# A hybrid decoder layer on one core: the weight ring's pool, the dt chain, the sparse rows and the ada sums change places

## The chip, the cores and the metric

The kernel runs on one core of a Trainium2 chip. The metric is device time in microseconds, from the start to the end of one execution; the number given for a kernel is the median of several runs. A core has five engines with a queue of instructions each, which run in order: PE (TensorE, matrix multiplication into PSUM), DVE (VectorE), ACT (ScalarE), POOL (GpSimd) and SP (SyncE, which here only issues transfers). An engine that reaches an instruction whose input is not there waits, and all behind it in its queue waits too. PEld is TensorE's weight load.

## The reference

One layer over 512 tokens of width 2048, in float32:

```
mod = silu(c) @ W_ada + b_ada            # six vectors of 2048: sh1, sc1, g1, sh2, sc2, g2
h = rmsnorm(x) * (1 + sc1) + sh1
c_q, c_kv, k_rope, z, xBC, dt_raw = split(h @ W_in)
attn = rmsnorm(MLA attention over c_q, c_kv, k_rope)      # 8 heads, causal
dt = softplus(dt_raw + dt_bias); cs = cumsum(-exp(a_log) * dt) inside chunks of 128
ssm = grouped rmsnorm(SSD over xBC, dt, gated with z)      # 16 heads, 4 chunks
x = x + g1 * (concat(attn, ssm) @ W_out)
h2 = rmsnorm(x) * (1 + sc2) + sh2
# PEER: 8 heads, each with two sets of 128 sub-keys
q = h2 @ W_query; top 16 of 128 in each half; top 16 of the 256 sums -> 16 of 16384 experts
x = x + g2 * sum over the chosen experts of gate * gelu(u_e . h2) * v_e
```

## The kernel before

Activations lie with features on the 128 partitions and the 512 tokens along the row. A float32 product is made of three matmuls: each factor is split into a rounded high part and a low rest (`mm`, lines 134 to 137). Weights come through a ring: `wload` (139 to 149) takes a raw buffer, loads it on SP's queue, makes the high part on ACT (147) and the low part with `sub_lo` on POOL or DVE (130, 148). `big` (151) calls it for eight rows of tiles at a time. The ring's pool is replaceable (`wpool`): "wp" with 4 raw and 2 + 2 part buffers of 4 KB up to line 766, "we" with 5 raw and 3 + 3 after it.

The stages, in the order of the program text: the first norm and the six latent tiles of w_in (274 to 316), rotary tables and latents (319 to 368), the late tiles of w_in (374 to 394), the projections of the first four heads (729), three weaves of attention, SSD, first half of w_out and the rest (731 to 735), the second half of w_out (739 to 748), the second norm (753 to 766), product-key selection (814 to 847), the spread of gates into a dense table (943 to 944), early expert rows (945), sparse rows (947 to 955), and the main loop over 128 groups of experts (1029 to 1059).

A framework orders each engine's queue: it takes the program text's order as priority and fills an engine with the first instruction that its timing model takes to be ready. So an instruction may run long before or after its place in the text. `tc.issue_after(ins)` puts what follows behind a given instruction of the same engine; `pace` holds the last matmul, the last DVE step and so on for that.

Pools are stacks on two sides of the on-chip memory. A pool that is opened after another was closed takes over its addresses, and a tile there waits for the old tiles that it overlaps (`reuse_waits="tile"`). At line 766 the left side is closed down to the constants; on it had stood, in this order, the ring "wp" (32 KB a partition), the small tiles of "ep" (9 KB), 28 pages of "pb" (2 KB each, among them the 16 tiles x1), and "tpp" with the norm's tiles h2t and h2k.

The ada stream. `ada_stream` (232 to 271) is a generator that computes 16 pieces of the vector `mod` on DVE: eight loads of 512 KB each per piece into two buffers (240, on SP), a multiplication with accumulation per half load (263, 265), and at step 3 of the next piece the sum over partitions, which is four transposes on PE (`colsum`, 172, tile adat), a reduction (174) and `ada_done`. Each step is pulled by `next(later)` after a piece of other work.

The dt chain (563 to 597) turns the dt columns of w_in into dt, adt, and by two small matmuls csp (588) and csl (592) into cumulative sums; SSD needs its results.

Selection (780 to 847): per query half a w_q tile, an evacuation qt (831), four score matmuls scp (834), five DVE searches per 128 tokens (839 to 843); per head a second round over the 256 sums, `cand` (786 to 795), and one-hot sums (809 to 812). The copies of h2 for the main loop into h2hi and h2lo are lines 844 and 845.

The spread (909 to 939): for groups of 32 tokens, one-hot tiles oi and oj on DVE, POOL and ACT, matmuls gps (930), copies gt on ACT (933) and writes of gd to memory from ACT's queue (937). The first 160 tokens (NS) are not computed densely; their rows of h2, written to memory as h2b in the norm (761), come back transposed as h2t and h2x (947 to 955): five loads on ACT's queue (950), 32 transposes h2p (954), eight copies (955). The main loop reads gd back as gc on SP (1035), between the loads of expert weights; x1s, loaded at 770, is the residual to which it adds from line 1057 on.

## Time and profile before

| | |
|---|---|
| time, median of 3 runs | 3273.81 us (3272.5 to 3276.46) |
| the profiled execution | 3275.95 us, its span 3274.2 us |
| busy share of the span | PE 93%, PEld 86%, DVE 78%, ACT 36%, POOL 30% |
| from about 1391 us to the end | the main loop, PE without a pause |

The profile is of one execution. A timeline row has start and duration in us, engine, line, operation, output and inputs, shapes and count; in square brackets the idle time of the engine ahead of it and what ended that. SPq and ACTq are transfers issued from the queues of SP and ACT. A table by stretches gives the busy time of every engine in each stretch, the granted clock of TensorE (1.00 is 2.4 GHz, 0.50 is 1.2 GHz) and the share and rate of the transfer engines. A row of the waits says which engine and line waited for which, the sum in us, how often, and the longest.

### The profile page before, as it was taken

The numbers are of one execution on the slowest core, as the hardware profiler recorded it, in microseconds if no ns is written. First come the engines' busy times: TensorE is split into PE (matmuls) and PEld (weight loads), VectorE is DVE, ScalarE is ACT, GpSimd is POOL, SyncE is SP. The second block draws the span as 40 slices with busy tenths as digits, with TensorE's granted clock in tenths as the row PEclk, the third lists the DMA queues.
The fourth block names the chain that finished last, engine by engine and source line by source line (L and its number), as shares of the span: only waits on it lengthen the run. The fifth ranks groups of instructions, "written<-read, shape, count | busy, mean of one in ns | idle before, by whom it ended". The sixth has DMA issues, their size and how long they took to land.

```text
span 3274.2 us, 46175 instructions
## 1 busy us (share of the span) xinstructions
PE 3058.9 (93%) x17753; PEld 2804.6 (86%) x17753; DVE 2539.3 (78%) x3844; ACT 1172.0 (36%) x1796; POOL 994.9 (30%) x701
## 2 busy tenths in 40 slices
PE   5998988889949989799999999999999999999999
PEld 2476766567837789799999999999999999999999
DVE  3257677787749999678888888888888888888885
ACT  2242235642242248633333333333333333333332
POOL 1143335544435665422222222222221121211210
PEclk8999999999969999899999999999999999999999
DMA  8636753438642236879998998998998998998994
GB/s 317 244 98 218 238 193 105 127 106 303 205 134 83 89 109 182 228 278 374 340 340 319 351 339 321 346 345 321 346 340 329 341 339 330 339 342 331 338 332 130
DMA packets 286844, 858.78 MB, mean 262 GB/s; under 512 B 35872, under 2 KB 96416, under 8 KB 245664
## 3 DMA queue, kind: packets, MB, share of 16 engines
q1 hardware_dynamic: 169024, 480.13, 41.7%
q0 software_dynamic: 46080, 335.56, 27.5%
q10 hardware_dynamic: 71520, 40.15, 4.2%
q8 instruction: 139, 2.28, 0.3%
q14 instruction: 81, 0.66, 0.1%
HBM read 816.65 MB, written 39.06 MB: 261 GB/s over the span
## 4 chain that ended last, share of the span: by engine, by line
PE 58%; DVE 6%; ACT 3%; DMA 1%; issue 1%; POOL 1%; ACTq 1%; SPq 0%; DVEq 0%; POOLq 0%
PE pv L137 10%; PE pv L135 10%; PE pv L136 10%; PE up L137 9%; PE up L135 9%; PE up L136 9%; ACT gt L933 1%; PE gps L930 1%; DMA gd<-gt 1%; DVE eq L809 0%; DVE slots L812 0%; DVE topi L843 0%; DVE sc L841 0%; DVE topi L840 0%; ACT oi L922 0%
## 5 line engine op out<-in xcount | busy, mean ns | idle before, releaser
L137 PE MATMUL up<-h2hi,ul 128*128 128x352 f32 x2048 | 665.3, 325 | 0.1
L135 PE MATMUL up<-h2hi,uh 128*128 128x352 f32 x2048 | 663.5, 324 | 0.4 <-ACT uh L147 0.4
L135 PE MATMUL pv<-ah,vh 128*128 128x352 f32 x2048 | 659.6, 323 | 3.1 <-ACT ah L1040 2.1
L136 PE MATMUL up<-h2lo,uh 128*128 128x352 f32 x2048 | 662.1, 323 | 0.0
L136 PE MATMUL pv<-al,vh 128*128 128x352 f32 x2048 | 661.0, 323 | 0.0
L137 PE MATMUL pv<-ah,vl 128*128 128x352 f32 x2048 | 657.1, 323 | 1.0 <-DVE vl L130 1.0
L147 ACT ACTIVATE vh<-vr 128x1024 fp32r<-128x1024 f32 x256 | 271.8, 1062 | 624.0 <-PE pv L136 539.2
L147 ACT ACTIVATE uh<-ur 128x1024 fp32r<-128x1024 f32 x256 | 271.4, 1061 | 557.8 <-PE up L136 418.5
L130 DVE TENSOR_TENSOR vl<-vr,vh 128x1024 fp32r<-128x1024 f32 x256 | 312.8, 1223 | 187.7 <-ACT vh L147 187.5
L130 POOL TENSOR_TENSOR wl<-wr,wh 128x1024 fp32r<-128x1024 f32 (+2 forms) x134 | 293.6, 2196 | 449.6 <-ACT wh L147 354.2
L130 DVE TENSOR_TENSOR ul<-ur,uh 128x1024 fp32r<-128x1024 f32 x230 | 281.3, 1223 | 145.5 <-ACT uh L147 145.5
L137 PEld LDWEIGHTS up<-h2hi,ul 128*128 128x128 f32 x2048 | 389.5, 190 | 0.4 <-DVE ul L130 0.4
L135 PEld LDWEIGHTS pv<-ah,vh 128*128 128x128 f32 x2048 | 385.6, 188 | 3.8 <-ACT ah L1040 2.5
L135 PEld LDWEIGHTS up<-h2hi,uh 128*128 128x128 f32 x2048 | 385.7, 188 | 0.7 <-ACT uh L147 0.7
L136 PEld LDWEIGHTS up<-h2lo,uh 128*128 128x128 f32 x2048 | 386.2, 189 | 0.0
L137 PEld LDWEIGHTS pv<-ah,vl 128*128 128x128 f32 x2048 | 384.6, 188 | 1.3 <-DVE vl L130 1.3
L136 PEld LDWEIGHTS pv<-al,vh 128*128 128x128 f32 x2048 | 385.4, 188 | 0.1
L981 POOL DMA_INDIRECT g<-u_r,idx x128 | 166.7, 1302 | 574.1 <-DVE acc L999 466.0
L981 POOL DMA_INDIRECT g<-v_t,idx x128 | 147.4, 1151 | 573.2 <-DVE pre L987 550.9
L999 DVE SCALAR_TENSOR_TENSOR acc<-g,cf,acc 128x2048 f32<-128x2048 f32 x127 | 297.8, 2345 | 0.0
L987 DVE CUSTOM_DVE_ANT_0 g<-g,h2t 128x2048 f32<-128x2048 f32 x128 | 292.1, 2283 | 2.4 <-DMA g<-u_r,idx 2.4
L147 ACT ACTIVATE wh<-wr 128x1024 fp32r<-128x1024 f32 (+2 forms) x134 | 126.7, 949 | 347.4 <-PE pj L136 76.4
(443 smaller groups left out, 4985.0 us busy)
## 6 DMA issues: line engine op xcount, KB each, us to landing
ur<-u_t SPq DMA_DIRECT2D x256, 512.0 KB, 6.6
vr<-v_d SPq DMA_DIRECT2D x256, 512.0 KB, 6.1
wada<-w_ada SPq DMA_DIRECT2D x128, 512.0 KB, 4.1
wada<-w_ada SPq DMA_DIRECT2D x128, 256.0 KB, 5.3
gd<-gt ACTq DMA_DIRECT2D x22, 1024.0 KB, 8.3
gc<-gd SPq DMA_DIRECT2D x32, 704.0 KB, 8.5
wr<-w_in SPq DMA_DIRECT2D x40, 512.0 KB, 4.9
wr<-w_out SPq DMA_DIRECT2D x32, 512.0 KB, 5.7
```

What stands on the lines that cost most here:

```text
L130: return eng.tensor_tensor(lo, src, hi.bitcast(F32), ALU.subtract)
L135: nc.tensor.matmul(ps, a[0], b[0], start=start, stop=False)
L136: nc.tensor.matmul(ps, a[0], b[1], start=False, stop=False)
L137: pace[5] = nc.tensor.matmul(ps, a[1], b[0], start=False, stop=stop)
L147: nc.scalar.activation(hi[:, :n], raw[:, :n], AF.Copy)
L930: pace[2] = nc.tensor.matmul(ps[:, t * P:(t + 1) * P], oi[:, t], oj[:, t], start=True, stop=True)
L933: nc.scalar.activation(gt[:, :, t4_ * 4:t4_ * 4 + 4].rearrange("p j t -> p t j"), pv_[:, :, jh * 64:(jh + 1) * 64], AF.Copy)
L981: nc.gpsimd.indirect_dma_start(out=g, out_offset=None, in_=table, in_offset=bass.IndirectOffsetOnAxis(ap=ix[:, s - s0:s - s0 + 1], axis=0))
L987: nc.vector.tensor_tensor_reduce(g, g, rows, 1.0, 0.0, ALU.mult, ALU.add, accum_out=pre[:, s:s + 1])
L999: nc.vector.scalar_tensor_tensor(acc, g, cf[:, s:s + 1], acc, op0=ALU.mult, op1=ALU.add)
```

## The change

Five things. The new ring's pool "we" is opened ahead of "p5", and x1s is no tile of "p5" any more: it is allocated, and loaded, in the main loop's pool. The dt chain stands behind the latents, ahead of the late tiles of w_in. The sum of an ada piece is made at step 6 of the next piece, not 3. The sparse rows are read after the second of three spread tiles, with a buffer of their own (one) in place of the three of gt. And cand and qt get a second buffer.

```diff
-            if i % 8 == 3 and ended:
+            if i % 8 == 6 and ended:
                 with tc.issue_after(pace[5].ins):
                     ada_done(*ended[:2], colsum(ended[2], "ada"))
...
     cq = latent(cq, "qa", 512, "rq")
+    def stile(name):
+        return ep.tile([P, NT, 16], F32, name=name)
+    dt, ax, ay, az, adt = stile("dt"), stile("ax"), stile("ay"), stile("az"), stile("adt")
...
+    nc.scalar.activation(sdec, sdec, AF.Exp)
...
-    (the same lines, from def stile to sdec, ahead of ys, rS)
...
     left.close()
+    wpool.update(pool=ctx.enter_context(pool("we")), raw=5, parts=3)
     p5 = ctx.enter_context(pool("p5"))
-    wpool.update(pool=ctx.enter_context(pool("we")), raw=5, parts=3)
-    x1 = p5.tile([P, KD, TD], F32, name="x1s")
-    nc.scalar.dma_start(x1, x1d[:, :, NS:].rearrange("k p t -> p k t"))
     h2 = [p5.tile([P, KD, TD], F32R, name=n) for n in ("h2hi", "h2lo")]
...
-        cand = lp.tile([P, NT, 16, 16], F32, tag="cand", name="cand", bufs=1)
+        cand = lp.tile([P, NT, 16, 16], F32, tag="cand", name="cand")
...
-        qt = lp.tile([P, T], F32, tag="qt", name="qt", bufs=1)
+        qt = lp.tile([P, T], F32, tag="qt", name="qt")
...
+    def sparse_rows():
+        for dst, t0, n in ((h2t, 0, P), (h2x, P, XT)):
+            h0 = rp.tile([P, KD, P], F32, name="h2f", bufs=1)
+            for q in range(P // n):
+                nc.scalar.dma_start(h0[:, :, q * n:(q + 1) * n], h2b[:, :, t0:t0 + n].rearrange("k p t -> p k t"))
+            for q in range(4):
+                ps = gpp.tile([P, T], F32, tag="g", name="h2p")
+                for j in range(4):
+                    nc.tensor.transpose(ps[:, j * P:(j + 1) * P], h0[:, q * 4 + j], ident)
+                nc.scalar.activation(dst[:, q * T:(q + 1) * T], ps, AF.Copy)
     for tt in (1, 2, 3):
         spread(tt, by_slot(tt))
+        if tt == 2:
+            sparse_rows()
     ges = {j: up(j) for j in range(EARLY)}
-    (the old loop over h2t and h2x, with tag="gt", bufs=3)
...
     pe_ = ctx.enter_context(pool("pe", 2))
+    x1 = pe_.tile([P, KD, TD], F32, name="x1s", bufs=1)
+    nc.scalar.dma_start(x1, x1d[:, :, NS:].rearrange("k p t -> p k t"))
```

## Rows read from the trace of the kernel before

**Rows 1.** Stretches: us; busy PE, PEld, DVE, ACT, POOL; clock, DMA, GB/s.
```profile
920.00:940.00 20.00, 0.00 (x0) 0.00 (x0) 18.34 (x26) 10.88 (x18) 9.30 (x6) 0.50 0.35 102
...
1000.00:1020.00 20.00, 20.00 (x92) 16.31 (x91) 20.00 (x84) 5.56 (x9) 14.11 (x6) 1.00 0.26 88
...
1260.00:1280.00 20.00, 19.64 (x153) 19.36 (x152) 20.00 (x60) 18.66 (x44) 13.53 (x16) 1.00 0.54 163
```

**Rows 2.** Waits of PE, whole span: sum in us, times, longest.
```profile
PE wq L135 <- ACT wh L147: 41.0, 1, 41.0
...
PE adat L172 <- DVE acc L263: 15.6, 6, 5.5
PE h2p L954 <- DMA h2f<-h2b: 15.3, 1, 15.3
PE scp L834 <- ACT qt L831: 12.3, 3, 7.9
...
PE csl L592 <- DVE cs L589: 8.8, 1, 8.8
```

**Rows 3.** Timeline of SP, ACT and PE around the first w_q tiles.
```profile
930.32 1.62 SPq L146 DMA_DIRECT2D wr<-w_q  x2
...
937.16 0.48 ACT L844 ACTIVATE h2hi<-h2h 128x352 fp32r<-128x352 f32 x1
...
949.50 1.65 ACT L147 ACTIVATE wh<-wr 128x512 fp32r<-128x512 f32 x3
...
950.17 0.79 PE L135 MATMUL wq<-h2h,wh 128*128 128x512 f32 x1 [41.03 <-ACT wh L147]
...
972.99 0.58 ACT L831 ACTIVATE qt<-wq 128x512 f32<-128x512 f32 x1
```

**Rows 4.** Timeline of DVE and POOL in the second norm.
```profile
920.33 0.42 DVE L763 CAST h2h<-h2k 128x512 fp32r<-128x512 f32 x1
...
921.29 1.47 DVE L763 CAST h2h<-h2k 128x512 fp32r<-128x512 f32 x1
...
924.00 0.42 DVE L763 CAST h2h<-h2k 128x512 fp32r<-128x512 f32 x1
...
938.65 1.27 POOL L130 TENSOR_TENSOR h2l<-h2k,h2h 128x512 fp32r<-128x512 f32 x1 [1.49 <-DVE h2h L763]
```

**Rows 5.** Timeline of DVE and PE: dt chain, first projections.
```profile
206.90 0.23 DVE L583 SCALAR_TENSOR_TENSOR adt<-dt,ea 128x64 f32<-128x64 f32 x1
...
459.02 1.54 DVE L263 SCALAR_TENSOR_TENSOR acc<-wada,ca,acc 128x512 f32<-128x512 f32 x2 [0.88 <-DMA wada<-w_ada]
...
461.50 0.68 DVE L464 TENSOR_REDUCE sk__3226<-sq 128x4 f32<-128x512 f32 x1
...
464.68 1.09 PE L436 MATMUL tf<-ident,kn 128*128 128x128 f32 x4
```

**Rows 6.** Waits of SP's queue, 262 to 460 us.
```profile
SPq L240 <- DVE acc L263: 120.3, 56, 4.9
```

**Rows 7.** Timeline of ACT at the end of w_in.
```profile
433.23 1.06 ACT L147 ACTIVATE wh<-wr 128x1024 fp32r<-128x1024 f32 x1 [0.56 <-PE pj L136]
```

**Rows 8.** Timeline of ACT, SP and PE from spread to main loop.
```profile
1364.71 6.53 ACTq L937 DMA_DIRECT2D gd<-gt  x2
...
1374.38 4.14 ACTq L950 DMA_DIRECT2D h2f<-h2b  x2
...
1382.64 1.05 ACT L147 ACTIVATE vh<-vr 128x1024 fp32r<-128x1024 f32 x1
...
1385.48 7.12 SPq L1035 DMA_DIRECT2D gc<-gd  x2
...
1391.53 1.54 PE L135 MATMUL pv<-ah,vh 128*128 128x352 f32 x4 [2.06 <-ACT ah L1040]
```

**Rows 9.** Line 955: durations in ns (least, median, most), first and last start.
```profile
L955 ACT ACTIVATE h2t<-h2p x4: 588/597/598, 1379.9 to 1384.1; 128x512 f32<-128x512 f32 x4
```

**Rows 10.** Transfers, 926 to 960 us: KB each, median us to landing.
```profile
x1s<-x1d ACTq DMA_DIRECT2D x1, 2816.0 KB, 11.9
```

More of the change, by code (lines that the diff above doesn't have):

```diff
@@ L368, in layer @@
     cq = latent(cq, "qa", 512, "rq")
+    def stile(name):
+        return ep.tile([P, NT, 16], F32, name=name)
+    dt, ax, ay, az, adt = stile("dt"), stile("ax"), stile("ay"), stile("az"), stile("adt")
+    nc.vector.tensor_tensor(ax, kd[:, :, 64:80], col("dtb")[:, None, :].to_broadcast([P, NT, 16]), ALU.add)
+    nc.scalar.activation(ay, ax, AF.Abs)
+    nc.scalar.activation(ay, ay, AF.Exp, scale=-1.0)
+    nc.vector.tensor_scalar(az, ay, 2.0, None, op0=ALU.add)
+    nc.vector.reciprocal(az, az)
+    nc.vector.tensor_tensor(ay, ay, az, ALU.mult)
+    nc.vector.tensor_tensor(az, ay, ay, ALU.mult)
+    nc.vector.tensor_scalar(dt, az, 1.0 / 15, 1.0 / 13, op0=ALU.mult, op1=ALU.add)
+    for n in (11, 9, 7, 5, 3, 1):
+        nc.vector.tensor_tensor(dt, dt, az, ALU.mult)
+        nc.vector.tensor_scalar(dt, dt, 1.0 / n, None, op0=ALU.add)
+    nc.vector.scalar_tensor_tensor(dt, dt, 2.0, ay, op0=ALU.mult, op1=ALU.mult)
+    nc.vector.scalar_tensor_tensor(dt, ax, 0.0, dt, op0=ALU.max, op1=ALU.add)
+    ea = ep.tile([P, 16], F32, name="ea")
+    nc.scalar.activation(ea, col("alog"), AF.Exp)
+    nc.vector.scalar_tensor_tensor(adt, dt, -1.0, ea[:, None, :].to_broadcast([P, NT, 16]), op0=ALU.mult,
+                                   op1=ALU.mult)
+    cs = ep.tile([P, 64], F32, name="cs")
+    ncs = ep.tile([P, 64], F32, name="ncs")
+    ps = psum2("csp")
+    nc.tensor.matmul(ps[:, :64], tri, adt.rearrange("p a b -> p (a b)"), start=True, stop=True)
+    nc.vector.tensor_copy(cs, ps[:, :64])
+    nc.vector.tensor_scalar(ncs, cs, -1.0, None, op0=ALU.mult)
+    ps = psum2("csl")
+    nc.tensor.matmul(ps[:, :64], ident[:, 127:128].to_broadcast([P, P]), cs, start=True, stop=True)
+    cdec = ep.tile([P, 64], F32, name="cdec")
+    nc.scalar.activation(cdec, ps[:, :64], AF.Exp)
+    sdec = ep.tile([P, 64], F32, name="sdec")
+    nc.vector.tensor_tensor(sdec, ps[:, :64], cs, ALU.subtract)
+    nc.scalar.activation(sdec, sdec, AF.Exp)
     gqk = ep.tile([P, 1], F32, name="gqk")
@@ L942, in layer @@
     ges = {}
+    def sparse_rows():
[8 more added lines that the diff above has]
+                nc.scalar.activation(dst[:, q * T:(q + 1) * T], ps, AF.Copy)
     for tt in (1, 2, 3):
         spread(tt, by_slot(tt))
+        if tt == 2:
+            sparse_rows()
     ges = {j: up(j) for j in range(EARLY)}
-    for dst, t0, n in ((h2t, 0, P), (h2x, P, XT)):
-        h0 = rp.tile([P, KD, P], F32, tag="gt", name="h2f", bufs=3)
-        for q in range(P // n):
-            nc.scalar.dma_start(h0[:, :, q * n:(q + 1) * n], h2b[:, :, t0:t0 + n].rearrange("k p t -> p k t"))
-        for q in range(4):
-            ps = gpp.tile([P, T], F32, tag="g", name="h2p")
-            for j in range(4):
-                nc.tensor.transpose(ps[:, j * P:(j + 1) * P], h0[:, q * 4 + j], ident)
-            nc.scalar.activation(dst[:, q * T:(q + 1) * T], ps, AF.Copy)
     gps.__exit__(None, None, None)
```

33 lines of the change are left out of this document (removed).

## The prediction

> **What bounds the kernel now.** I read the stretches first, then who TensorE waited for, then the timelines around the longest waits. From about 1391 us to the end TensorE never rests; the change does not touch that loop, so it can only bring its start forward. What decides is therefore the path to that start.
>
> The waits of TensorE [rows 2] name five places, and the change aims at every one: 41.0 us ahead of the first w_q matmul, 15.6 us in six ada sums, 15.3 us at the sparse rows (h2p), 12.3 us at the score matmuls (scp), 8.8 us at csl. They are not worth the same, because another engine may be what holds the path there.
>
> In the 41 us after the second norm begins TensorE does nothing and its granted clock is 0.50, the 1.2 GHz level, while VectorE is busy with the norm itself (first row of [rows 1]). Behind it lies product-key selection, where VectorE has no idle time at all (20.00 of 20 us, second row), then the spread, where VectorE is again at 20.00 and TensorE (19.64) and ScalarE (18.66) are nearly full (third row). So from the first top-8 search to the end of the spread VectorE sets the pace, and the whole block moves with its start. That start hangs on the first pair of w_q tiles.
>
> **Part 1, the weight ring.** In program order the change only swaps two pools and moves x1s out of the first; the effect is on addresses. Before, the ring began behind three tiles of 22,528 bytes, over pages that hold x1 and over the tiles of the norm, so its first load is issued at 930.32 [rows 3]. ScalarE then makes the 32 copies into h2hi and h2lo first (937.16 on) and converts the first weights only at 949.50; TensorE starts at 950.17 and the first query tile is evacuated at 972.99 [rows 3]. After the change the ring begins where the old ring stood (32 KB of its 44 KB); the rest lies on the small tiles of ep and on the first two pages of pb, which can hold x1 tiles. The old ring is free when w_out ends, before the norm, so the first weights can be loaded and converted before the first normed tile exists, and the scheduler, which fills an engine's queue by readiness in trace order, has no reason to put the copies ahead of them.
>
> TensorE then follows the norm. The last normed tile is complete at 938.65 + 1.27 = 939.9 [rows 4]. What is left then is the last k of one tile and four k of the other, 15 of 96 matmuls; at the 22.8 us that the whole pair took (950.17 to 972.99) that is 3.6 us, so the pair ends at 943.5 instead of 973.0: **29.5 us** as the upper end.
>
> Against it stands GpSimd. A cast of the norm takes 0.42 us alone and 1.47 us while GpSimd subtracts [rows 4]; with the ring open early, about six weight subtractions (the other two fall ahead of the norm) run beside the norm and can each hold up one more cast: 6 x 1.05 = 6.3 us, leaving 23.2. I take the middle, **-26 us**. The Trainium skill, SBUF — State Buffer, section "SBUF: two separate sides", says that VectorE in its two-port modes and GpSimd take their shared port as an exclusive lock for a whole instruction; the pair of durations agrees, and by that rule alone the gain would be 23 us, without it 29.5.
>
> The lower end is a ring of which one slot still waits for an x1 page: the third low-half slot lies on the two pages. If such a page is read last, TensorE has some 80 of 96 matmuls left at about 937, 19 us, and ends at 956: **-16 us**. Clock: TensorE trickles during the norm and may stay at 1.2 GHz; it waits for the norm anyway, so only the last 15 matmuls would pay, about 3 us, inside these ends.
>
> **Part 2, the dt chain.** It is moved in the trace, but its VectorE work already runs early: adt is written at 206.90 [rows 5], far ahead of its old place. What moves is two small matmuls with their copies. The 8.8 us at csl go, but their cover goes too: VectorE is then still multiplying ada rows, each waiting for its load, until 460.5, and only afterwards reduces the key squares (461.50) that the next TensorE step needs (464.68) [rows 5]. TensorE would wait there instead of at csl. I take **-1 us** (0.2 to 0.7 us of VectorE copies and the csl matmuls leave the chain); ends -2 and +1, the latter for ScalarE's table loads in the earlier place.
>
> **Part 3, the ada sums.** Three stream steps later is about one w_in tile later on TensorE, more than the longest wait of 5.5 us [rows 2], so five of the six waits go. But the stream does not depend on TensorE: the load queue (SP) waits 120.3 us between 262 and 460 us for VectorE to release an ada buffer [rows 6], and weight loads stand behind those waits. At the end of the stage the last weights are converted at 433.23 after only 0.56 us of waiting for TensorE [rows 7]: a TensorE that arrives earlier finds no weights. What it does gain is eaten by the same VectorE backlog as in part 2. One sum lies later, in the w_out stage, about 1.5 us of the 15.6. I take **-1 us**, ends -6 and +1.
>
> **Part 4, sparse rows and x1s.** At the end of the spread ScalarE issues the last two gd writes (1364.71, 6.53 us), then the sparse reads (two of five take 4.14 us of its queue), and converts v weights at 1382.64 only after them; the gc load stands on SP behind the v load that waits for this conversion, goes out at 1385.48, and TensorE resumes at 1391.53 [rows 8]. Without the sparse rows the conversion could run at about 1372; gc then waits for the last gd write instead, which I put at 1377 (6 us after its issue ends): **-8 us**, ends -10 and 0. Moved in front of the last spread tile, the work costs there 8 copies of 0.6 us = 4.8 us [rows 9], five issues, about 8 us by the pair above, and 32 transposes. ScalarE's spare time is 20 - 18.66 = 1.34 us in 20 [rows 1], some 4 us over the last tile, so at most 9 us come out; where VectorE is the pace, nothing does. I take +5, so **-3 us** for this part, ends -10 and +9.
>
> The x1s read (2816 KB, 11.9 us to land before [rows 10]) loses its quiet place at 936. Issued in the last spread tile it hides; behind the last gd write it shares the transfer engines with gc. The Trainium skill, DMA: Bandwidth & Descriptors, section "Issuing engines are not separate DMA queues", says that transfers of all queues interleave on the same engines, so ScalarE's queue gives no path of its own; no row of before shows these two together. By that the tail would lose up to 11.9 us more; this is a rival below.
>
> **Second buffers** for qt and cand: the 12.3 us at scp fall where VectorE is at 20.00 of 20, so they cover nothing and give nothing: 0, ends -4 (casts and searches reordered) and +1.
>
> **Sum:** -26 - 1 - 1 - 3 = -31 us. The profiled run took 3275.95 us (span 3274.2), 2.1 us above the median of 3273.81; 3275.95 - 31 = 3245, on the median's scale **3243 us**.
>
> **The rivals.**
> Ring half open (one low slot or one conversion behind the norm): -16 in place of -26, 3253 us. For it: the slot on the two pages; against: only one slot of eleven lies there.
> Ring without gain: the conversions stay behind the 32 copies in ScalarE's queue, as now (949.50 after 937.16 [rows 3]); TensorE starts at 950 as before and parts 2 to 4 remain: 3269 us, no measurable change. Against: the copies came first only because the weights were late.
> The early waits pay in full: 15.6 + 8.8 - 2 = 22 us more, 3221 us, if the load queue's order changes so that the ada stream ends earlier. Against: [rows 6, 7].
> x1s ahead of gc: +11.9 on the tail, 3255 us; as above.
> Slower: conversions of the next quarter stand in ScalarE's queue ahead of the norm's own steps and wait for TensorE to release a buffer, so norm and matmuls take turns. A quarter is two periods of 3.67 us of the norm (920.33 to 924.00 [rows 4]), 7.3 us; then two conversions (0.6 and 1.3 us each), 3.8 us; then 24 matmuls, 5.7 us at the pace of the pair above and twice that, 11.4 us, at the half clock granted there [rows 1]. Four such quarters of 22.5 us from 910 end at 1000, 27 us later than the 973 of now: 3276 + 27 - 5 = 3298 on the profiled scale, 3296 us on the median's. It costs time from 15.8 us a quarter (63 us over four). Against: three buffers give a lead of one and a half quarters.
>
> **How the numbers follow.** About 0.2% (6.5 us) is what a measurement here can tell from no change. Forecast 0.64; half open 0.10; x1s ahead of gc 0.06; early waits in full 0.06; no gain 0.09; slower 0.05. Faster: 0.64 + 0.10 + 0.06 + 0.06 = 0.86; same 0.09; slower 0.05. The range takes the forecast with the ends of its terms (not all at once) and the two rivals beside it: 3225 to 3264.
>
> **What would show it.** Right: w_q loads issued before 910, the first w_q matmul within some 5 us of the norm's first tile, the first query tile evacuated near 947 (973 - 26), VectorE without idle time from there to the end of the spread; adat and csl gone from the waits, and a wait at tf up to about 464 in their place; the main loop starting near 1360 (1391 - 31). Wrong: a first w_q matmul after 945; ScalarE idle inside the norm for TensorE; the spread longer by more than 9 us; gc landing behind x1s; the ada stream ending well before 460.

## The result and the profile after

The changed kernel takes 3295.16 us (median of 4 runs, 3292.3 to 3297.74), the kernel before 3273.15 us in the same comparison: ratio 1.0067, 95% interval 1.005 to 1.0085. It is slower by 22 us where 31 us less were forecast. The profiled execution of after has a span of 3295.1 us. One of the ten runs of e9_sp below took 9614.61 us; it is not in that kernel's ratio, and the median of the other nine is 3266.02 us in place of 3267.34.

The waits of TensorE after the change, whole span; columns as in [rows 2]:

```profile
PE wq L135 <- ACT wh L147: 34.0, 1, 34.0
...
PE tf L472 <- DVE rkm L163: 14.8, 1, 14.8
PE pv L135 <- ACT ah L1045: 13.5, 1, 13.5
...
PE adat L172 <- DVE acc L263: 9.7, 3, 4.4
```

Of the waits in [rows 2] csl and h2p have left the head of the list and adat fell by 5.9 us, yet nothing came of it. The wait for the first w_q weights, the largest, lost only 7.0 us (41.0 before). No new wait in this list explains 22 us, because what grew is for the most part not a wait of TensorE: it had expert rows (up) to do while another engine stood still.

So I cut the span into stages, by the first and last start of a tile in each trace. The table has the length of each stage in us: **w_in to w_out** from the first tf matmul to the last wob matmul; **ring** from the norm's first tile (h2k) to the first query tile (qt); **selection** from there to the last slots; **spread** from the first gps matmul to the last gt copy; **tail** from there to the first pv matmul; **main loop** from the first to the last pv matmul. The kernels of the experiments stand in it too.

| kernel | w_in to w_out | ring | selection | spread | tail | main loop |
|---|---|---|---|---|---|---|
| before | 436.6 | 62.4 | 219.7 | 163.7 | 27.1 | 1869.3 |
| after | 448.0 | 55.8 | 219.2 | 190.7 | 13.1 | 1871.6 |
| e1_ring | 437.6 | 53.2 | 225.2 | 161.6 | 26.5 | 1868.3 |
| e2_rows | 439.3 | 57.0 | 219.8 | 189.7 | 12.9 | 1871.0 |
| e3_ada | 445.8 | 61.9 | 220.3 | 162.2 | 27.4 | 1869.2 |
| e4_dt | 434.8 | 62.3 | 219.8 | 164.0 | 27.4 | 1868.9 |
| e5_split | 434.0 | 56.7 | 220.2 | 178.0 | 15.5 | 1870.4 |
| e6_pair | 432.9 | 36.0 | 227.2 | 160.9 | 27.0 | 1870.4 |
| e7_pool | 454.4 | 55.5 | 219.8 | 190.5 | 13.4 | 1870.1 |
| e8_x1s | 432.1 | 57.0 | 222.1 | 161.5 | 27.0 | 1871.1 |
| e9_sp | 435.2 | 55.7 | 220.3 | 170.3 | 15.3 | 1870.1 |
| e10_rest | 436.2 | 55.6 | 218.1 | 161.6 | 26.8 | 1870.9 |
| e11_pairx | 437.3 | 38.6 | 233.6 | 159.5 | 26.8 | 1870.5 |
| e12_hold | 448.1 | 51.8 | 219.2 | 189.3 | 13.0 | 1870.9 |
| e13_all | 437.9 | 38.3 | 219.3 | 166.8 | 16.2 | 1871.7 |
| e14_ring | 438.9 | 37.5 | 220.2 | 169.6 | 15.3 | 1872.4 |

Before to after: +11.4 from w_in to w_out, -6.6 in the ring, -0.5 in the selection, +27.0 in the spread, -14.0 in the tail, +2.3 in the loop. With +2.2 ahead of the first tf that is +21.8, against 3295.1 - 3274.2 = 20.9 of the spans; the rest, -0.9, lies in the short gaps between the stages.

**The spread.** Stretches of after at the place where the last spread tile should begin; columns as in [rows 1]:

```profile
1300.00:1320.00 20.00, 19.34 (x134) 18.75 (x134) 5.88 (x21) 12.28 (x26) 2.40 (x1) 1.00 0.87 250
1320.00:1340.00 20.00, 13.74 (x67) 12.89 (x68) 1.33 (x5) 7.56 (x13) 10.10 (x6) 0.74 0.72 141
```

VectorE, which filled the third row of [rows 1], works 7.2 of these 40 us. The timeline of after tells why (start, duration, engine, line, operation, in brackets the idle time before it and what ended that):

```profile
1314.58 3.98 ACTq L947 DMA_DIRECT2D h2f<-h2b  x1
...
1318.59 5.62 ACTq L947 DMA_DIRECT2D h2f<-h2b  x3
...
1336.36 1.91 PE L951 MATMUL h2p<-ident,h2f 128*128 128x128 f32 x16
1338.10 0.49 PE L903 MATMUL trp<-ident,slots 128*128 128x128 f32 x3
...
1338.63 0.56 DVE L905 COPY ijg<-trp 128x384 f32<-128x384 f32 x1 [32.75 <-PE trp L903]
```

Read it from the bottom. VectorE waits 32.75 us for the transposes (trp) of the last spread tile. These are three small matmuls whose data have long been there, but TensorE runs its queue in order, and ahead of them stand the 16 transposes of the second sparse tile. Their four reads could go out only when the first sparse tile had left the one buffer (h2f; its last transposes start at 1310.05); ScalarE issued them from 1314.58 to 1324.2, behind two gd writes. The last of them, issued at 1322.36, took 6.2 us to land, at 1328.5. That is not yet 1336.36, and TensorE is not idle ahead of these transposes: in its queue expert rows stood in front of them, and these had waited themselves for a conversion (uh) on ScalarE, which stood still behind the issue of the four reads:

```profile
1325.43 0.66 PE L135 MATMUL up<-h2hi,uh 128*128 128x352 f32 x1 [6.08 <-ACT uh L147]
```

So of VectorE's 32.75 us about 25 are the reads and their transposes, and the last 7.9 are expert rows that were in front.

**The ring.** The waits of SP's queue in after, 895 to 975 us, the longest first:

```profile
SPq L146 <- DMA h2b<-h2k: 30.5, 4, 21.5
```

And the timeline of SP, ScalarE and TensorE around the first w_q tiles of after:

```profile
937.93 35.59 SPq L146 DMA_DIRECT2D wr<-w_q  x12
...
951.12 0.48 ACT L843 ACTIVATE h2hi<-h2h 128x352 fp32r<-128x352 f32 x1
...
955.75 0.48 ACT L843 ACTIVATE h2hi<-h2h 128x352 fp32r<-128x352 f32 x1
956.14 0.61 ACT L147 ACTIVATE wh<-wr 128x512 fp32r<-128x512 f32 x1
...
956.80 0.79 PE L135 MATMUL wq<-h2h,wh 128*128 128x512 f32 x1 [33.98 <-ACT wh L147]
```

These rows answer [rows 3]. The first load is 13.7 us behind the norm's first tile (924.27) where it was 19.7 behind it; the last thing that it waited for was not memory but an h2b write of the norm, which landed at 937.87. The same holds for before, whose first load (930.32) went out when an h2b write had landed at 930.25. The waits of SP's queue in before, 895 to 975 us:

```profile
SPq L146 <- DMA h2b<-h2k: 35.4, 4, 27.5
```

ScalarE makes in after 13 copies into h2hi and h2lo between its last normed tile and the first conversion; before it made all 32.

**The tail.** The rows that answer [rows 8]:

```profile
1397.27 2.27 ACTq L936 DMA_DIRECT2D gd<-gt  x2
1399.57 3.63 ACTq L967 DMA_DIRECT2D x1s<-x1d  x1
...
1402.52 8.66 SPq L1040 DMA_DIRECT2D gc<-gd  x2
...
1410.10 1.54 PE L135 MATMUL pv<-ah,vh 128*128 128x352 f32 x4 [13.50 <-ACT ah L1045]
```

gc goes out 3 us after the last gd write has been issued, and the loop starts 7.6 us later.

### The profile page after: what moved, and what is told of

It is laid out like the page before. It is cut to its first block, busy times and chain, and to the rows that moved or that the text cites. A ratio compares the mean times of both kernels' runs of the same rounds, so it can differ in the third digit from the quotient of the medians.

```text
span 3295.1 us, 46166 instructions
## 1 busy us (share of the span) xinstructions
PE 3065.8 (93%) x17753; PEld 2809.5 (85%) x17753; DVE 2531.0 (77%) x3844; ACT 1172.9 (36%) x1796; POOL 994.0 (30%) x701
## 4 chain that ended last, share of the span: by engine, by line
PE 64%; DVE 11%; DMA 2%; issue 1%; ACT 1%; POOL 1%; ACTq 0%; SPq 0%; DVEq 0%; POOLq 0%
PE pv L135 10%; PE pv L137 10%; PE pv L136 10%; PE up L137 9%; PE up L135 9%; PE up L136 9%; DVE oj L927 2%; PE wob L137 1%; PE wob L135 1%; PE wob L136 1%; PE woa L137 1%; PE woa L136 1%; PE woa L135 1%; PE gps L929 1%; DVE eq L808 1%
## 5 line engine op out<-in xcount | busy, mean ns | idle before, releaser
L135 PE MATMUL pv<-ah,vh 128*128 128x352 f32 x2048 | 658.2, 323 | 15.5 <-ACT ah L1045 13.5
L135 PEld LDWEIGHTS pv<-ah,vh 128*128 128x128 f32 x2048 | 385.1, 188 | 16.2 <-ACT ah L1045 13.7
L263 DVE SCALAR_TENSOR_TENSOR acc<-wada,ca,acc 128x512 f32<-128x512 f32 x180 | 188.8, 1049 | 80.4 <-DMA wada<-w_ada 77.4
```

The source lines that it names most:

```text
L135: nc.tensor.matmul(ps, a[0], b[0], start=start, stop=False)
L263: nc.vector.scalar_tensor_tensor(acc, wt[:, kk], ca[:, k:k + 1], acc, op0=ALU.mult, op1=ALU.add)
```

## The experiments

Each kernel is compared with the kernel before on one chip; a ratio is that of its times to those of before, with its 95% interval.

### One part at a time: e1_ring, e2_rows, e3_ada, e4_dt

**e1_ring**: before, with the ring opened ahead of p5.

```diff
-    p5 = ctx.enter_context(pool("p5"))
     wpool.update(pool=ctx.enter_context(pool("we")), raw=5, parts=3)
+    p5 = ctx.enter_context(pool("p5"))
     x1 = p5.tile([P, KD, TD], F32, name="x1s")
```

> The kernel before with one edit, the ring opened ahead of p5; x1s keeps its place behind it. In the changed kernel the first w_q load went out at 937.93 although its memory had been free since 893; the built program makes it wait for the completion of an h2b write of the norm, and ScalarE stands eleven copies into h2hi and h2lo ahead of the first conversion. Theory (order): free memory does not bring the load ahead of those writes. In this build the first two conversions stand ahead of the copies, so the first load is issued some 14 us after the norm's first tile (910.6), near 924, the first w_q matmul comes near 938 to 942 in place of 950, the first query tile near 962 to 966 in place of 973, and the kernel takes 7 to 11 us less than before, about 3264. Prediction's theory: loads before 910, first query tile near 947, 26 us less, 3248. Rival (a ring gains nothing): first matmul at 950, same time as before.

Measured: 3263.73 us, ratio 0.9979 (0.9968 to 0.9989). The first load went out 13.7 us behind the norm's first tile, the first matmul 27.7 behind it (39.6 before), the query tile 53.2. The swap alone gains 9.2 us in the ring stage and gives 5.5 back in the selection. So a ring at this place is worth 7 us (0.0021 of 3272), not 26: the loads are still held, and TensorE waits 29.2 us. But here the first conversions come ahead of the copies on ScalarE, right behind the last normed tile. They did not wait for their load, which went out at 916.36, took 2.9 us and had landed 10.5 us before:

```profile
wr<-w_q SPq DMA_DIRECT2D x1, 256.0 KB, 2.9
...
929.76 0.63 ACT L147 ACTIVATE wh<-wr 128x512 fp32r<-128x512 f32 x1 [0.40 <-ACT h2k L760]
929.82 0.39 ACTq L770 DMA_DIRECT2D x1s<-x1d  x1
930.30 0.62 ACT L147 ACTIVATE wh<-wr 128x512 fp32r<-128x512 f32 x1
...
930.44 0.79 PE L135 MATMUL wq<-h2h,wh 128*128 128x512 f32 x1 [29.19 <-ACT wh L147]
```

**e2_rows**: before, with part 4 alone.

```diff
-    x1 = p5.tile([P, KD, TD], F32, name="x1s")
-    nc.scalar.dma_start(x1, x1d[:, :, NS:].rearrange("k p t -> p k t"))
...
     pe_ = ctx.enter_context(pool("pe", 2))
+    x1 = pe_.tile([P, KD, TD], F32, name="x1s", bufs=1)
+    nc.scalar.dma_start(x1, x1d[:, :, NS:].rearrange("k p t -> p k t"))
...
-        h0 = rp.tile([P, KD, P], F32, tag="gt", name="h2f", bufs=3)
+            h0 = rp.tile([P, KD, P], F32, name="h2f", bufs=1)
...
     for tt in (1, 2, 3):
         spread(tt, by_slot(tt))
+        if tt == 2:
+            sparse_rows()
```

> The kernel before with part 4 alone: sparse rows read ahead of the last spread tile, h2f with one buffer of its own, x1s loaded in the pool of the last stage. Theory (queue order): the transposes of the last spread tile (trp) stand on TensorE behind the sparse transposes, which wait for five reads issued on ScalarE's queue; VectorE then stands still some 33 us before its last tile in place of 4.5, so the spread ends 27 us later, and the tail between the last gt copy and the first pv matmul shortens from 27 to 12 or 13 us: in sum 11 to 14 us slower than before, 3285 to 3288. Prediction's theory: 5 us lost in the spread, 8 gained in the tail, 3 us less, 3270.

Measured: 3282.47 us, ratio 1.0033 (1.002 to 1.0046), 10 us slower. Spread 189.7, tail 12.9, and VectorE's wait ahead of the last tile is 31.40 us. Spread and tail are those of the changed kernel, so the spread's loss belongs to this part alone. The ring stage fell too, by 5.4 us, with no edit in it but x1s.

**e3_ada**: before, with `i % 8 == 6` in place of `i % 8 == 3` in the ada stream. **e4_dt**: before, with the dt chain in its new place.

> The kernel before with the ada sums at step 6 in place of 3, nothing else. Of the changed kernel 13.6 us were lost before the second norm (last wob matmul at 914.9, before 901.3), from two edits that could cause it, this one and the dt chain. Theory A (ada sums): the later sums move the row products of the w_out stage, last wob near 913, kernel 12 to 15 us slower, 3287. Theory B (dt chain): last wob near 901, time within 3 us of before. Prediction's theory: 1 us less, ends -6 and +1.

> The kernel before with the dt chain moved ahead of the late tiles of w_in, nothing else. Theory A (ada sums cost the 13.6 us ahead of the norm): last wob at 899 to 902, csl gone from TensorE's waits, a wait at tf in its place, time within 3 us of before. Theory B (dt chain costs it): last wob near 913, kernel 12 to 15 us slower, 3287. Prediction's theory: 1 us less, ends -2 and +1.

Measured: e3_ada 3280.34 us, ratio 1.0034 (1.0021 to 1.0046); e4_dt 3271.27 us, ratio 0.9998 (0.9988 to 1.0008). The stage from the first tf to the last wob is 445.8 us in the first and 434.8 in the second. Theory A holds: the ada sums cost it. It costs 9 us against the profile of before, 7 to 14 against the 432 to 439 us that this stage takes in the other kernels with the sums at step 3. The place is sharper than the stage: from the first to the last matmul of the first half of w_out (woa) it is 104.8 to 106.9 us in the twelve kernels with the sums at step 3 and 112.2 to 115.7 in the four with step 6. The stretch of woa in before, then in e3_ada; columns as in [rows 1]:

```profile
704.90:810.40 105.50, 101.21 (x507) 79.57 (x508) 86.00 (x102) 32.51 (x54) 41.04 (x16) 1.00 0.73 249
...
701.40:817.10 115.70, 103.98 (x504) 81.58 (x505) 82.35 (x102) 32.79 (x54) 41.01 (x16) 0.96 0.68 231
```

TensorE and VectorE there in e3_ada:

```profile
740.35 0.38 PE L670 MATMUL pc<-mask_t,identb 128*128 128x128 bf16 x4 [2.76 <-ACT ce L665]
742.79 1.54 DVE L263 SCALAR_TENSOR_TENSOR acc<-wada,ca,acc 128x512 f32<-128x512 f32 x2 [2.91 <-DMA wada<-w_ada]
744.25 0.69 DVE L678 TENSOR_TENSOR mt<-mt,cb 128x512 f32<-128x512 f32 x1
...
744.99 1.18 PE L684 MATMUL yp<-mt,xd 128*64 128x128 f32 x8 [4.26 <-DVE mt L678]
```

A step of the SSD (mt) stands on VectorE behind two ada row products, these wait 2.91 us for the load of a row, and TensorE waits 4.26 us for mt. In this stretch of before yp does not wait for mt at all. The two waits of TensorE shown here come to 7.0 us, and behind them its granted clock is at 0.50 (1.2 GHz) from 742 to 748 us, where it was 1.00 in the whole stretch of before. The changed kernel has the pair too (pc 2.8 us, yp 2.7). That the step of the sums sets where the row products stand among the SSD's steps follows from the single edit; why it puts them just there I did not trace.

### Why the ring gave so little: e7_pool, e6_pair, e8_x1s, e12_hold

**e7_pool**: the changed kernel with `nc.gpsimd.dma_start(h2b[d], hk[:, :NS])`, so that the h2b writes leave ScalarE's queue.

> The changed kernel with the h2b writes on GpSimd's queue in place of ScalarE's. In the built program the first w_q loads then wait for x1 stores of the stage before and not for h2b writes. Theory (both): the loads are held by the completion of h2b writes, the conversions by ScalarE's order (13 copies into h2hi and h2lo stand ahead of the first one). So the first w_q load goes out before the norm's first tile or within 3 us of it, in place of 13.7 us behind it, and yet the first w_q matmul comes 31 to 34 us after the norm's first tile as in the changed kernel (32.5); time as the changed kernel within 6 us, 3290 to 3300. Rival (loads alone): the early loads bring the first matmul to 15 to 25 us behind the norm's first tile, 8 to 17 us less than the changed kernel. Rival (memory): the load still goes out 13 us behind the norm's first tile.

Measured: 3293.26 us, ratio 1.0058 (1.0038 to 1.0078). The first w_q load went out at 914.93, 7.3 us ahead of the norm's first tile (922.25), and there is no wait for h2b left on SP. The first matmul came 33.5 us behind the norm's first tile, no better than with the late load (32.5):

```profile
949.27 0.48 ACT L843 ACTIVATE h2hi<-h2h 128x352 fp32r<-128x352 f32 x1
...
955.06 0.61 ACT L147 ACTIVATE wh<-wr 128x512 fp32r<-128x512 f32 x1
```

Two holds in a row, and taking away the first alone brings nothing. The first load had been issued 40 us before its conversion; ScalarE finished the norm and then made copies, 15 of them ahead of the first conversion.

**e12_hold**: the changed kernel, the copies of a head behind that head's scores in ScalarE's queue.

```diff
-        nc.scalar.activation(sc, ps.rearrange("p (a b) -> p a b", a=NT), AF.Copy)
+        isc = nc.scalar.activation(sc, ps.rearrange("p (a b) -> p a b", a=NT), AF.Copy)
...
+        with tc.issue_after(isc.ins):
             nc.scalar.activation(h2[0][:, hj], act[hj][0][:, NS:], AF.Copy)
             nc.scalar.activation(h2[1][:, hj], act[hj][1][:, NS:], AF.Copy)
```

> The changed kernel with one edit: the copies of a head into h2hi and h2lo come in ScalarE's queue behind that head's score copy (sc); nothing else is moved. All ten first conversions then stand ahead of every copy. Theory (ScalarE's order): the first conversion follows the last h2k (26 us behind the norm's first tile) at once, the first w_q matmul comes 26 to 29 us behind the norm's first tile in place of 32.5, the first query tile at 50 to 53 in place of 55.8, the first search 6 to 7 us later, and the kernel takes 3 to 6 us less than the changed kernel, 3289 to 3292. Prediction's theory in full (free memory brings the matmuls beside the norm): query tile at 35 or earlier. Rival (loads): the loads, issued from 13.7 us on and held by h2b writes, land too late for it, query tile at 55 or later, no gain.

Measured: 3287.44 us, ratio 1.0052 (1.0035 to 1.007). First matmul at 27.7, query tile at 51.8 us behind the norm's first tile: 3.9 us less than in the changed kernel, as the theory of ScalarE's order has it (the two kernels' ratios to before, 1.0052 and 1.0067, overlap in their intervals). So the copies were in the way, for this small part of the 26 us:

```profile
946.18 0.81 ACT L761 ACTIVATE h2k<-h2t,modT 128x512 f32<-128x512 f32 x1 [0.48 <-DVE h2t L759]
...
947.40 0.63 ACT L147 ACTIVATE wh<-wr 128x512 fp32r<-128x512 f32 x1 [0.40 <-ACT h2k L761]
...
954.89 0.63 ACT L147 ACTIVATE wh<-wr 128x512 fp32r<-128x512 f32 x1 [5.08 <-PE wq L136]
```

The first conversion follows the last normed tile at once. What is left is the pair itself: 24.1 us of matmuls, all of them behind the norm. No run takes away both holds, on loads and on copies, from the changed kernel; e6_pair, which traces the pair inside the norm on the old ring, comes below.

**e8_x1s**: before, with x1s alone moved to the last pool (the x1 lines of e2_rows' diff).

> The kernel before with x1s alone moved, from p5 at the norm to the pool of the last stage behind the spread. In e2_rows the time from the norm's first tile to the first query tile fell from 62.4 to 57.0 us with no other edit near it. Theory A (x1s): the x1s read shares the transfer engines and the queue with the first w_q loads, and its absence gives these 5 us; at the tail the read (27.6 us to land in the changed kernel) does not hold gc, so the tail stays at 27 us: 4 to 6 us less than before, 3267. Theory B (rival of the prediction): issued behind the last gd write it shares the engines with gc and with the sparse reads, and the tail grows by 6 to 12 us: slower than before by 1 to 7.

Measured: 3266.15 us, ratio 0.9979 (0.9968 to 0.999). Ring stage 57.0, tail 27.0. The numbers are Theory A's: moving the x1s read away from the norm gives 5.4 us in the ring stage, as much as in e2_rows. Its reason is not shown: the first load went out 20.9 us behind the norm's first tile, no earlier than before (19.7). What the trace of e8_x1s shows is that the first conversion stands behind 13 copies, as in the changed kernel, and not behind 32. The two edits do not add: x1s alone gives 5.4 us, the ring alone 9.2 (e1_ring), both 6.6 in the changed kernel, where 13 copies are back in front of the first conversion; in e1_ring there are none. Behind the spread the x1s read took 19.0 us to land and held nothing up, but here it went out at 1381.3, behind the first gc read (1377.4), so this run does not test the rival of x1s ahead of gc.

**e6_pair**: before, with the first w_q pair traced inside the norm, on the old ring.

```diff
+    wqs = [psum("wq"), psum("wq")]
     for d in range(KD):
...
         act.append(a)
+        if d % 4 == 3:
+            for n in range(2):
+                big(wqs[n], w_q[n], act, k0=d - 3, k1=d + 1, first=(d == 3), last=(d == KD - 1), step=4)
     left.close()
```

> The kernel before with the first pair of w_q tiles traced inside the norm's loop, four k at a time, on the old ring; pools and order behind it as before. Theory (order): the loads are traced ahead of the norm's end, stand on SP among the x1 stores and wait for no h2b write, and their conversions stand in ScalarE's queue inside the norm, ahead of the copies into h2hi and h2lo; the first w_q matmul comes some 12 us after the norm's first tile, the first query tile is evacuated within 5 us of the norm's last tile, some 32 us after the norm's first tile in place of 62: 22 to 30 us are gained there, and since VectorE sets the pace from the first search on, the kernel takes 20 to 28 us less, 3244 to 3252. Rival (turn-taking): conversions and matmuls inside the norm delay it; query tile at 45 us or later, gain under 15 us. Rival (weights): the second pair's ring, which still opens behind x1 and the norm, is then what TensorE waits for; the first search comes early but the selection is longer by 10 to 20 us, and the kernel gains 5 to 15.

Measured: 3250.95 us, ratio 0.9937 (0.9919 to 0.9956): 23 us less than before. The first loads go out among the x1 stores (873.5), the conversions stand ahead of the norm and inside it, and the query tile follows the norm's last tile by 5 us:

```profile
937.87 0.81 ACT L761 ACTIVATE h2k<-h2t,modT 128x512 f32<-128x512 f32 x1 [0.89 <-DVE h2t L759]
...
939.16 0.63 ACT L147 ACTIVATE wh<-wr 128x512 fp32r<-128x512 f32 x1
...
943.25 0.60 ACT L831 ACTIVATE qt<-wq 128x512 f32<-128x512 f32 x1 [3.46 <-PE wq L137]
```

The ring stage is 36.0 us, 26.4 less than before: the very gain that I had forecast, from an edit that does put the work there. Of it 7.5 us go again in the selection, where VectorE waits 5.4 us for its second search (the 10.6 us named in an expectation below are its wait ahead of the first): the rival of the second pair's weights holds in part.

```profile
960.10 0.87 DVE L839 MAX8 tops<-sc 128x8 f32<-128x128 f32 x4 [5.44 <-ACT sc L836]
```

### Why the spread grew, and whether it need: e5_split, e9_sp

**e5_split**: part 4, with the two sparse tiles apart. **e9_sp**: the same, the sparse reads on SP's queue. The lines against e2_rows:

```diff
-        if tt == 2:
-            sparse_rows()
+        if tt < 3:
+            sparse_rows([((h2t, 0, P), (h2x, P, XT))[tt - 1]])
...
-                nc.scalar.dma_start(h0[:, :, q * n:(q + 1) * n], h2b[:, :, t0:t0 + n].rearrange("k p t -> p k t"))
+                nc.sync.dma_start(h0[:, :, q * n:(q + 1) * n], h2b[:, :, t0:t0 + n].rearrange("k p t -> p k t"))
```

The last pair of lines is e9_sp's alone.

> Part 4 alone, as in e2_rows, but with the two sparse tiles apart: h2t's transposes after the first spread tile, h2x's after the second, so that h2x's four reads have a whole spread tile to land in the one buffer. The work is the same. In e2_rows the spread (first gps matmul to last gt copy) took 189.7 us in place of 163.7. Theory (wait): of these 26 us nearly all is the wait of VectorE and TensorE for h2x's reads behind h2t's transposes; with the reads early the spread takes 168 to 174 us, the tail stays at 13, and the kernel takes 3272.3 - 14 - 5 (the ring stage, as in e2_rows) + 4 to 10, 3257 to 3264. Rival (work): the copies, transposes and the issue of reads on ScalarE's queue cost the 26 us themselves; spread 185 or more, 3278 or more.

> As e5_split, with the five sparse reads issued on SP's queue in place of ScalarE's. In e5_split the spread took 178.0 us, 14.3 more than before and 11.7 less than e2_rows; ScalarE stood 7.7 us at its one-hots (oi) while its queue issued reads, TensorE waited 7.9 us for these and VectorE 7.9 us for TensorE, and 7.8 us for the transposes of the next tile. Theory (issue): ScalarE's queue, busy issuing, costs about 8 of the 14 us; with the reads on SP the spread takes 168 to 172 us, the tail stays at 13 to 16, and the kernel takes 5 to 9 us less than e5_split, 3262 to 3268. Rival (work): copies and transposes cost it, spread 176 to 180, same time as e5_split. Rival (SP blocked): the weight loads queue behind the reads on SP, which wait for the buffer, and the spread is longer than 180.

Measured: e5_split 3272.71 us, ratio 1.0 (0.9988 to 1.0013); e9_sp 3267.34 us, ratio 0.999 (0.998 to 1.0001). The spread takes 178.0 and 170.3 us, against 189.7 in e2_rows and 163.7 before. The wait of VectorE ahead of the last tile is 5.11 and 4.29 us in place of 31.40. So of e2_rows' 26.0 us, 11.7 went with the tiles apart, 7.7 with the reads off ScalarE's queue, and 6.6 are left; that these are the work itself is not shown. Each term is from one trace, and the spread takes 159.5 to 164.0 us in the eight kernels where its text is that of before. No run gives h2f a second buffer in the changed order, so the buffer and the place in the text are not told apart. The wait that went away in e9_sp, among ScalarE's of e5_split in the spread:

```profile
ACT oi L920 <- issue: 7.7, 1, 7.7
```

e5_split fell between its two theories (174 and 185), since I had counted the issue as work. By their times e5_split and e9_sp are not told apart; the terms are read from the stages. Even with 170.3 the move is worth only 163.7 + 27.1 - 170.3 - 15.3 = 5 us, and e9_sp's time is not better than that of e8_x1s, which has x1s alone.

### What the two losing edits cost, and versions that keep the rest: e10_rest, e11_pairx, e13_all, e14_ring

**e10_rest**: the changed kernel with ada sums and sparse rows as before.

> The changed kernel with two of its edits undone: ada sums at step 3 again, sparse rows at their old place again. The ring, the x1s load in the last pool, the dt chain and the second buffers stay. Theory (the two edits are the loss): the stage from the first tf to the last wob matmul takes 435 to 438 us as before (448 in the changed kernel), the spread 162 to 165, the tail 27, and the ring stage 55.5 to 57 from the norm's first tile to the first query tile, as in the changed kernel and in e8_x1s, 62.4 before; in sum 6 to 9 us less than before, 3264 to 3268. Rival (something else in the change costs): 3272 or more. If the ring swap gives anything beyond x1s's move, the ring stage is under 55.

Measured: 3262.85 us, ratio 0.9975 (0.9963 to 0.9986). First stage 436.2, spread 161.6, tail 26.8. With those two edits undone the change gains 8 us; with them it loses 22. What else is in it costs nothing in sum.

**e11_pairx**: e6_pair with e8_x1s and e4_dt.

> Three edits together on the kernel before: the first w_q pair traced inside the norm on the old ring (e6_pair, 23 us less), x1s moved as in e8_x1s (6 to 8 us less), the dt chain moved as in e4_dt (nothing measured). In e6_pair the x1s read went out at 945.6, where the second pair's weights load, the selection took 227 us in place of 220, and VectorE waited 10.6 us for its second search. Theory (x1s is the second hold): with x1s away the selection takes 220 to 223, and the kernel 3243 to 3248, 4 to 7 us less than e6_pair. Rival (ring): the second pair still waits for its ring or for ScalarE's copies; selection 226 or more and no gain beyond e6_pair, 3250.

Measured: 3260.47 us, ratio 0.9973 (0.996 to 0.9986): worse than e6_pair alone. Both expectations of what would follow are wrong in place: the loss is ahead of the first search, which comes 51.1 us behind the norm's first tile (42.7 in e6_pair). VectorE's wait ahead of the second search did fall, from 5.4 to 2.7 us, but from the first search on the selection is no shorter (221.1 and 220.5 us), and I did not follow why. ScalarE again:

```profile
950.37 0.60 ACT L830 ACTIVATE qt<-wq 128x512 f32<-128x512 f32 x1 [2.68 <-PE wq L137]
952.53 0.50 ACT L843 ACTIVATE h2hi<-h2h 128x352 fp32r<-128x352 f32 x1 [1.56 <-PE wq L136]
...
961.84 0.48 ACT L843 ACTIVATE h2hi<-h2h 128x352 fp32r<-128x352 f32 x1
962.23 0.57 ACT L835 ACTIVATE sc<-scp 128x512 f32<-128x512 f32 x1
```

With x1s out of the way the copies can start early, and they slip in between the query tile and its scores.

**e13_all**: before with the edits of e6_pair, e8_x1s, e9_sp and e12_hold. **e14_ring**: e13_all with the ring ahead of p5.

> The kernel before with four edits: first pair inside the norm (e6_pair), x1s moved (e8_x1s), sparse tiles apart with reads on SP (e9_sp), copies behind sc (e12_hold). In e11_pairx 13 pairs of copies stood between the first query tile and its scores, and the first search came 12.4 us after the query tile in place of 6.7. Theory (copies): with them out of the way the first search comes 6 to 7 us after the query tile, at 43 to 45 us from the norm's first tile (69.2 before, 51.0 in e11_pairx), the selection from there takes 213 to 219 us; with 170 in the spread and 15 in the tail, TensorE's main loop starts 447 to 458 us after the norm's first tile in place of 480.9: 23 to 34 us less than before, 3238 to 3249. Rival (weights of the second pair): the second search waits for them, selection 221 or more, 3250 or more.

> e13_all with the ring opened ahead of p5, as in the change. Theory: behind the first pair the ring's place matters little, since it is the second pair's loads that use it: they can go out when the old ring's weights of the first pair are read, so within 4 us of e13_all either way. Rival (ring early pays): the second pair's weights come 5 to 10 us earlier and the selection is shorter by as much; 3233 to 3243. Rival (ring takes the old ring's slots): second pair's loads wait for the first pair's matmuls, selection 5 us longer.

Measured: e13_all 3243.66 us, ratio 0.9912 (0.9891 to 0.9933); e14_ring 3245.24 us, ratio 0.9918 (0.9896 to 0.994). With the copies held back the gains stand together: 28 us less than before, 51 less than the changed kernel, by the medians. The first search comes 46.7 us behind the norm's first tile, later than expected (43 to 45), since the scores of the first tile came 7.7 us behind qt: TensorE had w_q matmuls in front of them. The ring's place is worth nothing that can be measured once the first pair is in the norm: the two ratios overlap.

## Why the prediction was wrong, point by point

**What bounds the kernel.** Right: the main loop was not touched (1871.6 and 1869.3 us), and only its start moved. The loop is some 2 us longer in the kernels that load x1s behind the spread (1870.1 to 1872.4; the others 1868.3 to 1870.4), which I had not counted; I did not look for its cause.

Three terms of the sum failed, each by 10 us or more: part 1 gave 6.6 in place of 26, part 3 cost 9 (e3_ada) to 11 (after) where it was to give 1, and part 4 cost 13.0 (27.0 in the spread, 14.0 back in the tail) where it was to give 3. Without the losses of parts 3 and 4 the sign is right (e10_rest); with part 1 as forecast the loss would by the sum have been 22 - 19 = 3 us.

**Part 1, the ring, -26: the step that failed** is "The old ring is free when w_out ends, before the norm, so the first weights can be loaded and converted before the first normed tile exists, and the scheduler ... has no reason to put the copies ahead of them". It took the place of the ring in memory for what held the first load of before (930.32), where the SP waits of before show h2b writes (35.4 us). Free memory alone changed little: in the changed kernel the loads stood behind h2b writes (30.5 us in SP's waits), and the conversions behind the whole norm and 13 copies. ScalarE's order alone was enough to keep the gain away: with early loads the first matmul came 33.5 us behind the norm's first tile (e7_pool), and without copies in front 27.7 (e12_hold), still behind the last normed tile. Whether the hold on the loads alone would have been enough is not shown. The ends (-29.5, -16) were both ends of the assumption that the work moves; none priced the case that it stays (and the -16 should be -17: 973 less 956). The size was right: where the pair is traced inside the norm, it gains 26.4 (e6_pair). So was the price of GpSimd beside the norm: the norm's first to last h2k took 25.8 us before and 30.7 in e6_pair, 4.9 longer, where I had put 6.3 at most. That rests on VectorE's rows, which leave it idle for about 1 us in this norm: the 16 casts and 24 other passes took 34.1 us there and 30.5 before, with six weight subtractions of GpSimd beside them as forecast. It was not the casts that they held up, as I had thought (0.75 us in the mean, 0.88 before), but the other passes (h2t 0.93, 0.69 before). The Trainium skill, SBUF — State Buffer, section "SBUF: two separate sides", which I had cited for this, agrees in direction.

The rival "ring without gain" looked at the right queue, ScalarE's, and gave that 9%; its argument against ("the copies came first only because the weights were late") is what e7_pool refutes. The weights were early, and 15 copies still came first. But the copies are the small part (3.9 us, e12_hold); that the conversions stand behind the whole norm was in no rival. One of the prediction's signs of being wrong came here: a first w_q matmul after 945 (956.8); another in part 4, a spread longer by more than 9 us.

**Part 2, the dt chain, -1.** Right: e4_dt is at 0.9998, csl is gone, and in its place TensorE waits at tf, as forecast (10.4 us in e4_dt, 14.8 in after). That it does so until 466.86, near the forecast of 464, is luck in part, since this stretch takes 456.2 to 466.8 us in kernels with the same text:

```profile
466.86 1.09 PE L472 MATMUL tf<-ident,kn 128*128 128x128 f32 x4 [14.78 <-DVE rkm L163]
```

**Part 3, the ada sums, -1 (ends -6 and +1).** Wrong in sign and place. That the waits in w_in would gain nothing was right; three adat waits are left, 9.7 us. But I looked only at the waits that the edit removes and priced the w_out stage by its one sum (1.5 us). There the same stream shares VectorE with the SSD's last steps, in an order that the edit changes, and 9 us came out. The step that failed is that a later sum has no effect beyond its own wait; the question to ask of a step that is moved is which queue it is moved past.

**Part 4, sparse rows and x1s, -3.** The tail gained 14.0, not 8: gc went out 5.5 us behind the last gt copy (1397.0 to 1402.5), where I had put 12.6 (1364.4 to 1377). The last gd issue took 2.27 us in place of 6.53, and gc followed it after 3.0 in place of 6. In the spread I had counted five issues, eight copies and "at most 9" (by the pair of issues that I named, 4.14 us for two, five are 10.4 and not 8, so it should have been 11): 6.6 are left in e9_sp. The step that failed is that only busy time was priced, and no wait. The second tile's reads cannot start before the first has left the single buffer, and in TensorE's in-order queue the transposes of that tile, with expert rows in front, stand ahead of trp, for which VectorE waits. VectorE was the engine that I had named as the pace of this stage; in e2_rows a wait of 31.40 us put ahead of its input made the spread 26.0 us longer. The rival of x1s ahead of gc came, but small: the first gc read took some 1.5 us more to land than before, not 11.9, and 3.6 more in e5_split and e9_sp (8.5 us). Transfers of after issued from 1402 to 1403 us, then of before from 1385 to 1386, KB and median us to landing, to be held against [rows 10]:

```profile
x1s<-x1d ACTq DMA_DIRECT2D x1, 2816.0 KB, 27.6
gc<-gd SPq DMA_DIRECT2D x1, 704.0 KB, 6.5
...
gc<-gd SPq DMA_DIRECT2D x1, 704.0 KB, 4.9
```

The rule that I had cited there (The Trainium skill, DMA: Bandwidth & Descriptors, section "Issuing engines are not separate DMA queues") agrees with these rows: both reads were slower beside each other. It was the large one that paid most (27.6 us in place of 11.9), where nothing waited for it.

**Second buffers, 0.** The selection took 219.2 us (219.7 before): that agrees, though no run has these buffers alone.

**The rivals and the range.** Slower by over 0.2% had 5%, with a mechanism (turn-taking of norm and conversions) that did not happen. The two things that did happen, in parts 3 and 4, were inside my terms, but with upper ends too low: +1 where +9 to +11 came, and +9 for the spread where +27 came.

## What to carry to other kernels

Free memory does not bring a load forward: look at what stands ahead of it in trace order, and at every queue that its consumer shares; trace the work where it is to run, or put an order edge on what must stay behind. Before moving work with a wait in it, list what is queued behind it on each in-order engine and which of those feeds the engine that sets the pace: here 16 transposes, late by their reads and by the rows in front of them, held VectorE's input back, and with the issue of those reads that made 19 of the 26 us. When two holds lie in a row, an experiment that removes one can show nothing, so remove each alone and both.

## What the runs showed that I had not expected

A load on SP's queue waited for writes that ScalarE had issued, of other data: 30.5 us in four waits in after. In the program as built a transfer waits for the completion of an earlier one that signals on the same semaphore (the counter that tells of its landing), and the transfers of SP and ScalarE use the same eight: the load at 937.93 signals on that of the h2b write that landed at 937.87. With those writes on GpSimd's queue (e7_pool) the waits are gone, and the first load goes out 7.3 us ahead of the norm's first tile in place of 13.7 behind it.

Issuing four reads of 256 KB took ScalarE's queue 3.98 + 5.62 = 9.6 us in after, and the engine's own next work behind them waited 8.2 us for the issue:

```profile
1324.32 2.00 ACT L147 ACTIVATE uh<-ur 128x1024 fp32r<-128x1024 f32 x2 [8.24 <-issue]
```

The stretch ahead of the first tf took between 456.2 and 466.8 us in kernels whose text is the same there (e1_ring, e8_x1s). Differences of a few us in a span are therefore read here from the stages, not from the spans.
